# HGRN ahead of MoBA in the second mixer chain of a two-layer four-mixer decoder trunk, with longer delay estimates

## The chip, the cores and the metric

One core of a Trainium2 chip runs the whole program in one launch. The metric is the device time of one execution in microseconds (us). The kernel before takes 927.18 us, the median of three runs from 926.2 to 927.2 us.

Engine names as the profile uses them: PE is TensorE's matmul, PEld its weight load, DVE is VectorE, ACT is ScalarE, POOL is GpSimd, SP is SyncE.

## The reference

Two layers over 256 tokens of width 1024, float32, then a final RMSNorm. In each layer four token mixers of 4 heads of 64 work in parallel on projections of the same normed input, and each is projected, gated and summed:

```python
h = rms_norm(x, norm1_g[layer])
y_sb   = stick_breaking_attention(...)   # sigmoid attention with a reversed running product
y_rwkv = rwkv7_time_mix(...)             # S_t = S diag(w) + (S a) b^T + v k^T, per head
y_moba = moba_attention(...)             # one block of 256 here: causal softmax with partial rotary
y_hgrn = hgrn2_mixer(...)                # S_t = diag(f) S + (1-f) i^T, then RMSNorm and gate
for n, y_n in enumerate((y_sb, y_rwkv, y_moba, y_hgrn)):
    gate = sigmoid(h @ w_gate[n])
    merged += gate * (y_n @ w_branch[layer, n])
x = x + merged @ w_out[layer]
h2 = rms_norm(x, norm2_g[layer])
x = x + (silu(h2 @ w_ffn_gate) * (h2 @ w_ffn_up)) @ w_ffn_down
```

## The kernel before

Every large projection is done in split precision: `split` (lines 126 to 129) makes a rounded part `hi` of a float32 weight on ACT (line 128) and the remainder `lo` on DVE (line 129), and `mm3` (line 119) issues three fp32r matmuls for one product. A weight tile is 128x1024 (512 KB), loaded into one of four `raw` buffers by SP and split when its unit begins. The results of units go to the PSUM tiles `pa`, of which there are three.

The mixer phase of a layer, `phase`, gives PE two kinds of work. **Units** are projections, gates and branches, generators that yield every three or six matmuls. **Streams** are the mixers themselves, generators that issue a step of small matmuls and the vector work behind it and then yield a number: an estimate in ns of how long that vector work takes. `drive` (line 86) merges them. It counts the matmul time issued so far in `pe[0]`, and a stream whose step yielded `lat` is taken up again only when

```python
s[0] = pe[0] + lat * LATK        # LATK = 1.7
```

has been reached; until then the next units are issued. The estimates so set how many unit matmuls stand on PE between two steps of a mixer. They appear in no instruction.

There are two streams in a layer. The first, `rwkv` (line 471), makes scores by pairs of heads (`pair_scores`, line 535), inverts triangular blocks of 16 on DVE (`product`, lines 587 to 597), sends blocks through DRAM by two DMAs that ACT issues (`tri`, lines 600 and 603), solves the larger blocks with small matmuls, and applies the state in two chunks `c`. The second, `rest` (line 1085), runs stick-breaking attention `sba`, then `moba`, then `hgrn`. `hgrn` prepares keys and queries on DVE (lines 822 to 834) and goes through seven levels: at each, 16 or fewer small matmuls use `key` and `Q`, and DVE then updates `Q` (line 868, twice), `key` (line 869) and evicts the scores (line 876), before the next level's matmuls may begin. `moba` rotates q and k on DVE and POOL (lines 981 to 984), scores, softmax (lines 930, 991 to 998), transposes (`flip_att`, line 938) and weighs.

The order of the instructions on each engine is then made by the framework's scheduler from the order in which the program issues them. Each engine works its instructions off in that order.

Of the kernel before, what the change touches and what calls it, by code (L numbers as in the profile page):

```python
# [46 lines left out]
def trunk(ctx, tc, x, w_t, w_n, w_br, w_out, w_gu, w_dn, par, lora, rows, gains, consts, masks, out):  # L47
# [9 lines left out]
    def sb(tag, width, dt=F32):  # L57
        return mx.tile([128, width], dt, name=tag, tag=tag, bufs=NB[tag])

    def ps(tag):  # L60
        return psum.tile([128, 512], F32, name=tag, tag=tag, bufs=NB[tag])

    def g2d(t, a):
        return t.rearrange("p (a t) -> p a t", a=a)
# [130 lines left out]
    for i in range(20):  # L195
        nc.tensor.matmul(warm[:, 0:256], flat1[:, 0:128], flat1[:, 0:256], start=True, stop=True)
        if i in (8, 12):
            c = (i - 8) // 4
# [266 lines left out]
    def rwkv(m, l, yT):  # L465
# [100 lines left out]
        for c in range(2):  # L566
            LK.append(g2d(sb("b1", 1024), 4))
            pair_scores(kh, LK[c], c)
            yield 2400
        yield 500  # L570
        nc.vector.tensor_copy(yb.rearrange("p s t -> p (s t)")[:, 1::34],
                              xb.rearrange("p s t -> p (s t)")[:, 1::34])
        tmp = sb("xy", 512)[0:64]
# [157 lines left out]
        for c in range(2):  # L731
            p = ps("p1")
            for hp in range(2):
                for a in (2 * hp, 2 * hp + 1):
                    d = slice(a * 64, (a + 1) * 64)
                    mm_cols(p[:, d], LK[c][:, a, 0:128], vn[:, c, d], a == 0, c == 0 and a == 3)
                if c:
                    mm(p[:, hp * 128:(hp + 1) * 128], AR[:, 2 * hp + c, 0], st[:, hp], False, hp == 1)
            rh = sb("h1", 256)
            nc.scalar.copy(rh, p[:, 0:256])  # L740
            yield 1000
            p = ps("p1")
            for a in range(4):
                d = slice(a * 64, (a + 1) * 64)
                mm_cols(p[:, d], Y[c][:, a], rh[:, d])
            u = sb("h1", 256)
            nc.scalar.copy(u, p[:, 0:256])
            yield 1000
            if c == 0:
                p = ps("p1")  # L750
                for a in range(4):
                    o = p[hrow(a), (a // 2) * 64:(a // 2) * 64 + 64]
                    d = slice(a * 64, (a + 1) * 64)
                    mm(o, bkn[:, 0, d], u[:, d], True, False)
                    mm(o, bkn[:, 1, d], vn[:, c, d], False, True)
                st = g2d(sb("h1", 256), 2)
                nc.gpsimd.memset(st, 0.0)
                for hp in range(2):
                    for e in range(2):
                        s = hrow(e)  # L760
                        nc.vector.tensor_scalar(st[s, hp, s], p[s, hp * 64:(hp + 1) * 64], fac[s, hp:hp + 1],
                                                None, op0=OP.mult)
            p = ps("p1")
            for hp in range(2):
                for a in (2 * hp, 2 * hp + 1):
                    d = slice(a * 64, (a + 1) * 64)
                    mm_cols(p[:, d], LK[c][:, a, 128:256], vn[:, c, d], a == 0, False)
                if c:
                    mm(p[:, hp * 128:(hp + 1) * 128], AR[:, 2 * hp + c, 1], st[:, hp], False, False)
                for a in (2 * hp, 2 * hp + 1):  # L770
                    d = slice(a * 64, (a + 1) * 64)
                    mm_cols(p[:, d], LB[c][:, a, 128:256], u[:, d], False, a == 3)
            yv = g2d(p[:, 0:256], 4)
            mean = sm.tile([128, 4], F32, name="mean")
            nc.vector.tensor_reduce(mean, yv, axis=AX.X, op=OP.add)
            nc.vector.tensor_scalar(mean, mean, 1.0 / 64, None, op0=OP.mult)
            yc = sb("h1", 256)
            ycv = g2d(yc, 4)
            nc.vector.tensor_tensor(ycv, yv, bcast(mean, 64), op=OP.subtract)
            y2 = sb("h1", 256)  # L780
            nc.scalar.activation(y2, yc, AF.Square)
            var = sm.tile([128, 4], F32, name="var")
            nc.vector.tensor_reduce(var, g2d(y2, 4), axis=AX.X, op=OP.add)
            rsqrt_small(var, var, 1.0 / 64, 64e-5)
            nc.vector.tensor_tensor(ycv, ycv, bcast(var, 64), op=OP.mult)
            nc.vector.tensor_tensor(yc, yc, gnw, op=OP.mult)
            nc.vector.tensor_tensor(yc, yc, bonus[:, c], op=OP.add)
            nc.vector.tensor_tensor(yc, yc, g[:, c], op=OP.mult)
            ys.append(yc)
            yield 200  # L790
        yield 6000
        yT[1] = y_T(ys, "p1"), pe[0] + 2500

# [25 lines left out]
    def hgrn(m, l, yT):  # L819
# [22 lines left out]
        for lev in range(7):  # L842
# [19 lines left out]
            n = 4 * nb  # L862
# [36 lines left out]
        for t in range(2):  # L899
# [13 lines left out]
            nc.vector.tensor_tensor(y, y, gs[:, t], op=OP.mult)  # L913
            ys.append(y)
            yield 300
        yield 3500
        yT[3] = y_T(ys, "p2"), pe[0] + 2500

    def scores(q, k, t, mask):
# [57 lines left out]
    def moba(m, v, yT):  # L977
        r = []
        for u in m:
            o = g2d(sb("c2", 512), 2)  # L980
            nc.vector.stream_shuffle(o, g2d(u, 2), SWAP)  # L981
            nc.vector.tensor_tensor(o, o, over(sinT, 2), op=OP.mult)
            nc.gpsimd.tensor_tensor(g2d(u, 2), g2d(u, 2), over(cosT, 2), op=OP.mult)
            nc.vector.tensor_tensor(o, o, g2d(u, 2), op=OP.add)
            r.append(o)
        yield 5000
        po = ps("p3")
        for t in range(2):
            z, n = scores(r[0], r[1], t, cn[:, K_MO:K_MO + 128])
            mxs = sm.tile([128, 4], F32, name="mxs")  # L990
            nc.vector.tensor_reduce(mxs, z, axis=AX.X, op=OP.max)
            nc.vector.tensor_scalar(mxs, mxs, -0.125, None, op0=OP.mult)
            den = sm.tile([128, 4], F32, name="den")
            for a in range(4):
                nc.scalar.activation(z[:, a], z[:, a], AF.Exp, bias=mxs[:, a:a + 1], scale=0.125,
                                     accum_out=den[:, a:a + 1])
            nc.vector.reciprocal(den, den)
            nc.vector.tensor_tensor(z, z, bcast(den, n), op=OP.mult)
            yield 5000 + 2500 * t
            ts = []  # L1000
            flip_att(z, t, ts)
            yield 1200
            weigh(po, ts, t, v, 256)
        yT[2] = y_split(po), pe[0] + 2500
        yield 500
# [46 lines left out]
    def phase(hr, g, l, ws):  # L1052
        yT, gt, mg, mT = {}, {}, {}, {}
        streams, units = [], []
        yes = lambda: True

        def add(gen, ready=yes):
            units.append((ready, gen))

        def start(gen, pos):  # L1060
            def f():
                streams.append([pe[0] + 1500, gen, pos])
                streams.sort(key=lambda s: s[2])
                return
                yield
            add(f)

        vv = [sb("p", 512) for _ in range(2)]

        def use_v(t, p):  # L1070
            nc.scalar.copy(vv[t], p)

        h = norm_group(hr, g, ws, use_v)
        if l == 0:
            with tc.issue_after(tail[0].ins), tc.issue_after(tail[1].ins):
                setup()
            load_small()
        rm, sm_, mm_, hm = [], [], [], []
        for i in range(4):
            add(lambda i=i: rwkv_proj(h, l, i, rm))  # L1080
        start(rwkv_s(rm, l, yT), 0)
        for j in range(2):
            add(lambda j=j: copy_proj(h, l, 8 + 2 * j, sm_))

        def rest():
            yield from sba(sm_, vv, yT)
            while len(mm_) < 2:
                yield 2000
            yield from moba(mm_, vv, yT)
            while len(hm) < 4:  # L1090
                yield 2000
            yield from hgrn(hm, l, yT)
        start(rest(), 1)
        for j in range(2):
            add(lambda j=j: copy_proj(h, l, 12 + 2 * j, mm_))
        add(lambda: hgrn_proj(h, l, hm))
        cnt = [0, 0]
        for n in (0, 2, 3, 1):
            for f in range(2):
                add(lambda n=n, f=f: gate_unit(h, l, n, f, gt), lambda: len(gt) < NB["gt"] // 2)  # L1100
                add(lambda n=n, f=f: branch_unit(l, n, f, cnt, yT, gt, mg, mT),
                    lambda n=n, f=f: n in yT and yT[n][1] <= pe[0] and len(gt.get((n, f), ())) == 2)

        ahead = []

        def fetch():
            ahead.extend(prefetch([("gu", l, 0, c) for c in (0, 1)]))
            return
            yield
        units.insert(len(units) - UPRE, (lambda: 1 in yT and yT[1][1] <= pe[0], fetch))  # L1110
        drive(units, streams)
        return mT, ahead, flip_unit(1, mg, mT)
# [184 lines left out]
```

## Time and profile before

| | |
|---|---|
| runs | 926.2, 927.18, 927.2 us (median 927.18) |
| the profiled execution | 927.26 us, of which the span from first to last instruction is 925.5 us |
| PE busy | 905.9 us, 98% of the span, 5902 matmul passes |
| PEld | 758.4 us, 82% |
| DVE | 647.4 us, 70% |
| ACT | 475.2 us, 51% |
| POOL | 84.7 us, 9% |
| mean granted TensorE clock | 0.999 |
| DMA | 158.11 MB, mean 171 GB/s |

How to read it: busy shares are means over stages. The mixer phase of the first layer lies between about 17 and 254 us, that of the second between about 470 and 710 us; the merge and the FFN lie behind each. A row of the timeline gives start, duration, engine, line, operation, output and inputs, how many instructions are merged, and in brackets the idle time of the engine before it and what ended it. Matmuls overlap, so what one costs on PE is the distance from its start to the next start.

### The profile page before, as it was taken

Reading aid. Unit: us, or ns where it says so; the run is one execution under the profiler, and the core shown is the slowest. Engines: PE = TensorE matmul, PEld = TensorE weight load, DVE = VectorE, ACT = ScalarE, POOL = GpSimd, SP = SyncE. Lnnn points to the kernel's source line nnn. Section 1 sums busy time; section 2 is a strip of 40 time slices with the busy share of each in tenths; the row PEclk is TensorE's granted clock in tenths of the full one; section 3 lists DMA queues with packets and bytes.
Section 4 is the critical chain, followed back from the end, with each engine's and each line's share of the span. In section 5 each row is a group of like instructions: output and inputs, shape, how many; then the busy total and the mean of one; then the engine's idle time right before and its main releaser. Section 6 shows DMA issues by size and latency. Waiting matters only on the chain.

```text
span 925.5 us, 15008 instructions
## 1 busy us (share of the span) xinstructions
PE 905.9 (98%) x5902; PEld 758.4 (82%) x5902; DVE 647.4 (70%) x957; ACT 475.2 (51%) x726; POOL 84.7 (9%) x94
## 2 busy tenths in 40 slices
PE   8999999999999999999999999999999999999996
PEld 5999677778888888888889986777887888888885
DVE  6668877876766666668567778867778566666665
ACT  6564375355535455556345636644455445545453
POOL 3011100333000000000000201032230000000000
PEclk9999999999999999999999999999999999999999
DMA  8644453345864566667435544433467356656551
GB/s 308 222 147 152 121 169 128 102 155 176 266 205 138 181 190 196 182 204 267 144 115 160 161 138 144 142 123 124 131 211 253 112 184 204 189 184 195 182 182 46
DMA packets 50424, 158.11 MB, mean 171 GB/s; under 512 B 9393, under 2 KB 11953, under 8 KB 50354
## 3 DMA queue, kind: packets, MB, share of 16 engines
q1 hardware_dynamic: 43632, 155.19, 52.7%
q10 hardware_dynamic: 6722, 1.97, 0.9%
q8 instruction: 46, 0.75, 0.3%
q14 instruction: 24, 0.20, 0.1%
HBM read 154.91 MB, written 2.23 MB: 170 GB/s over the span
## 4 chain that ended last, share of the span: by engine, by line
PE 83%; DVE 8%; DMA 4%; issue 2%; ACT 2%; POOL 0%; SPq 0%; ACTq 0%; POOLq 0%; DVEq 0%
PE pa L80 58%; PE p L80 23%; DVE lo L129 2%; DMA raw<-in_w_n_dram 1%; PE p L89 1%; PE pa L89 1%; DMA h<-flat 1%; DMA tri<-yb 1%; DMA flat<-b 1%; DMA raw<-in_w_gu_dram 1%; DVE b L966 1%; ACT hi L128 0%; DVE b L542 0%; DVE c L129 0%; DVE c L981 0%
## 5 line engine op out<-in xcount | busy, mean ns | idle before, releaser
L129 DVE TENSOR_TENSOR lo<-raw,hi 128x1024 fp32r<-128x1024 f32 x268 | 330.2, 1237 | 162.6 <-ACT hi L128 159.7
L128 ACT CAST hi<-raw 128x1024 fp32r<-128x1024 f32 x268 | 279.1, 1048 | 238.5 <-PE pa L80 118.4
L80 PE MATMUL pa<-h,hi 128*128 128x256 f32 (+1 forms) x1280 | 277.9, 339 | 0.0
L80 PEld LDWEIGHTS pa<-h,hi 128*128 128x128 f32 x1280 | 215.9, 190 | 24.6 <-issue 2.0
L80 PE MATMUL pa<-hi,h 128*128 128x512 f32 x576 | 193.4, 400 | 2.2 <-DVE p L813 2.2
L80 PE MATMUL pa<-h,lo 128*128 128x256 f32 x960 | 179.9, 283 | 0.0
L80 PEld LDWEIGHTS pa<-h,lo 128*128 128x128 f32 x960 | 148.6, 191 | 7.0 <-issue 0.7
L80 PEld LDWEIGHTS pa<-hi,h 128*128 128x128 f32 x576 | 108.1, 188 | 27.6 <-DVE p L813 3.0
L80 PE MATMUL p<-hi,c 128*128 128x512 f32 (+1 forms) x352 | 113.4, 394 | 0.0
L80 PE MATMUL pa<-lo,h 128*128 128x512 f32 x288 | 112.7, 391 | 0.0
L80 PEld LDWEIGHTS p<-hi,c 128*128 128x128 f32 x352 | 66.1, 189 | 15.2 <-DVE c L129 0.6
L80 PE MATMUL p<-lo,c 128*128 128x512 f32 (+1 forms) x176 | 69.2, 393 | 0.0
L80 PEld LDWEIGHTS pa<-lo,h 128*128 128x128 f32 x288 | 54.2, 188 | 10.0 <-issue 0.3
L263 POOL TENSOR_TENSOR rs<-rs,half 128x1 f32<-128x1 f32 x10 | 6.0, 595 | 471.6 <-DVE rs L262 471.6
L80 PE MATMUL pa<-hi,y 128*128 128x512 f32 x128 | 43.9, 399 | 0.0
L80 PE MATMUL p<-hi,b 128*128 128x512 f32 x128 | 41.5, 396 | 0.2 <-DVE b L129 0.2
L80 PEld LDWEIGHTS p<-lo,c 128*128 128x128 f32 x176 | 33.1, 188 | 6.8
L1034 POOL TENSOR_TENSOR p<-p,gt 128x512 f32<-128x512 f32 x16 | 31.2, 1973 | 54.3 <-DVE gt L1032 54.3
L340 DVE TENSOR_TENSOR gt<-gt,pa 128x256 f32<-128x256 f32 x80 | 33.1, 414 | 0.0
L128 ACT CAST c<-xy 128x512 fp32r<-128x512 f32 x20 | 12.4, 620 | 39.2 <-DVE xy L1137 39.2
L339 ACT COPY gt<-pa 128x256 f32<-128x256 f32 x80 | 29.3, 366 | 0.0
L80 PEld LDWEIGHTS pa<-hi,y 128*128 128x128 f32 x128 | 24.0, 188 | 6.3 <-issue 1.0
(276 smaller groups left out, 936.5 us busy)
## 6 DMA issues: line engine op xcount, KB each, us to landing
raw<-in_w_gu_dram SPq DMA_DIRECT2D x88, 512.0 KB, 3.7
raw<-in_w_n_dram SPq DMA_DIRECT2D x80, 512.0 KB, 3.5
raw<-in_w_dn_dram SPq DMA_DIRECT2D x44, 512.0 KB, 3.5
raw<-in_w_t_dram SPq DMA_DIRECT2D x40, 512.0 KB, 3.6
raw<-in_w_br_dram SPq DMA_DIRECT2D x16, 512.0 KB, 3.6
raw<-in_w_out_dram SPq DMA_DIRECT2D x16, 512.0 KB, 4.4
b<-in_gains_dram SPq DMA_DIRECT2D x4, 512.0 KB, 5.2
flat<-b ACTq DMA_DIRECT2D x4, 256.0 KB, 3.2
```

Source lines behind the costliest of these rows:

```text
L80: nc.tensor.matmul(o, l, r, start=start, stop=stop)
L89: nc.tensor.transpose(o, i, ident)
L128: a = nc.scalar.copy(dst[0], src)
L129: return a, (eng or nc.vector).tensor_tensor(dst[1], src, dst[0], op=OP.subtract)
L263: nc.gpsimd.tensor_tensor(dst, dst, half[:, :dst.shape[-1]], op=OP.pow)
L339: nc.scalar.copy(dst, p[:, 256:512])
L340: nc.vector.tensor_tensor(dst, dst, p[:, 0:256], op=OP.add)
L966: nc.vector.tensor_tensor_scan(kb, kb, reset[t][:, ::-1], 1.0, op0=OP.mult, op1=OP.add)
L1034: e.tensor_tensor(mg[f, t], mg[f, t], g, op=OP.add)
```

## The change

Five delay estimates are altered, `rest` runs `hgrn` before `moba`, and the projections, gates and branches of the two change places likewise.

```diff
@@ rwkv: scores of k (LK), two steps
         for c in range(2):
             LK.append(g2d(sb("b1", 1024), 4))
             pair_scores(kh, LK[c], c)
-            yield 2400
-        yield 500
+            yield 3200
@@ rwkv: application of the state, chunks c = 0, 1
             ys.append(yc)
-            yield 200
+            yield 1500 - 1300 * c
         yield 6000
@@ hgrn: before the last transposes
             ys.append(y)
             yield 300
-        yield 3500
+        yield 4300
@@ moba: after the softmax of query half t
-            yield 5000 + 2500 * t
+            yield 6800 + 1500 * t
             ts = []
             flip_att(z, t, ts)
@@ phase
         def rest():
             yield from sba(sm_, vv, yT)
+            while len(hm) < 4:
+                yield 2000
+            yield from hgrn(hm, l, yT)
             while len(mm_) < 2:
                 yield 2000
             yield from moba(mm_, vv, yT)
-            while len(hm) < 4:
-                yield 2000
-            yield from hgrn(hm, l, yT)
         start(rest(), 1)
+        add(lambda: hgrn_proj(h, l, hm))
         for j in range(2):
             add(lambda j=j: copy_proj(h, l, 12 + 2 * j, mm_))
-        add(lambda: hgrn_proj(h, l, hm))
         cnt = [0, 0]
-        for n in (0, 2, 3, 1):
+        for n in (0, 3, 2, 1):
```

No instruction is added or taken away on PE, DVE, ACT, POOL or SP; the lines of the changed kernel from 570 on are one lower than those of the kernel before. What moves is best seen at three places. In these rows a number behind a name tells buffers apart, `lo<-raw,hi` is the DVE part of a weight's split, and `h_1078` and `h_1120` are the blocks that come back from DRAM for the inversion.

The first place is DVE in the first layer, from the arrival of the blocks for the inversion to the evictions of the scores of k, chunk 0 (line 542). Before:

```order
L129 TENSOR_TENSOR lo<-raw,hi 128x1024
L981 STREAM_SHUFFLE c_1150<-p 128x512
L981 STREAM_SHUFFLE c_1155<-p 128x512
L542 COPY_PREDICATED b_1122<-mk,p_1123 128x2x256
L542 COPY_PREDICATED b_1122<-mk,p_1124 128x2x256
L982 TENSOR_TENSOR c_1150<-c_1150,cn 128x512
```

Now:

```order
L570 COPY yb<-h_1078 64x8
L591 TENSOR_TENSOR xy<-yb,h_1078 64x4x4 x2
L594 TENSOR_REDUCE h_1260<-xy 64x4x2 x2
L591 TENSOR_TENSOR xy<-h_1260,yb 64x4x4 x2
L812 TENSOR_TENSOR p<-p,pa 128x256
L823 TENSOR_SCALAR c_1114<-p,lb_129,lb_128 128x256 x2
L825 TENSOR_SCALAR p<-p,lb_128,lb_127 128x256 x2
L828 TENSOR_TENSOR c_1119<-p,c_1114 128x512
L833 TENSOR_TENSOR b_1121<-p 64x2x256
L542 COPY_PREDICATED b_1080<-mk,p_1081 128x2x256
L542 COPY_PREDICATED b_1080<-mk,p_1082 128x2x256
L833 TENSOR_TENSOR b_1121<-p 64x2x256
```

HGRN's preparation (L823 to L833) stands where the shuffles of MoBA's rotation stood, and all of it is behind the copy that waits for the blocks.

The second place is DVE a little further on, around the last level of the inversion (the products of 64x512). Before:

```order
L542 COPY_PREDICATED b_1172<-mk,p_1173 128x2x256
L542 COPY_PREDICATED b_1172<-mk,p_1174 128x2x256
L592 TENSOR_TENSOR xy<-yb,h_1120 64x512
L595 TENSOR_REDUCE h_1227<-xy 64x64
L592 TENSOR_TENSOR xy<-h_1227,yb 64x512
L129 TENSOR_TENSOR lo<-raw,hi 128x1024
L595 TENSOR_REDUCE yb<-xy 64x8x8
L129 TENSOR_TENSOR lo<-raw,hi 128x1024
L813 TENSOR_TENSOR p<-p,pa 128x256
```

Now:

```order
L542 COPY_PREDICATED b_1155<-mk,p_1157 128x2x256
L591 TENSOR_TENSOR xy<-yb,h_1078 64x512
L871 TENSOR_TENSOR tot_1377<-tot_1326 128x64
L594 TENSOR_REDUCE h_1260<-xy 64x64
L129 TENSOR_TENSOR lo<-raw,hi 128x1024
L837 COPY dg<-p_1192 128x8
L867 TENSOR_TENSOR b_1121<-b_1121,p 64x2x128 x2
L868 TENSOR_TENSOR c_1114<-c_1114,p 128x256
L875 COPY_PREDICATED h_1203<-mk,p_1205 128x128
L591 TENSOR_TENSOR xy<-h_1260,yb 64x512
L129 TENSOR_TENSOR lo<-raw,hi 128x1024
L594 TENSOR_REDUCE yb<-xy 64x8x8
```

HGRN's update behind level 0 (L867, L868) now stands inside the inversion, behind one of its two large products; the matmuls of level 1 need it.

The third place is ACT around the DMA that writes the inverted blocks (`tri<-yb`), which waits for DVE's last reduction into `yb`. Before:

```order
L600 DMA tri<-yb 64x256
L811 COPY p<-pa 128x256
L812 ACTIVATE p<-pa 128x256
L603 DMA h_1356<-tri 128x8x16
L811 COPY p<-pa 128x256
L812 ACTIVATE p<-pa 128x256
L128 CAST hi<-raw 128x1024
```

Now:

```order
L950 COPY p<-pa 128x512
L599 DMA tri<-yb 64x256
L128 CAST hi<-raw 128x1024
L602 DMA h_1412<-tri 128x8x16
L128 CAST hi<-raw 128x1024 x2
L1011 ACTIVATE gt<-pa 128x512 x2
L128 CAST hi<-raw 128x1024 x4
```

The evictions of HGRN's token-major projection out of `pa` (L811, L812) stood behind both DMAs; they have moved far ahead of them, and splits and gate sigmoids stand there now.

## Rows read from the trace of the kernel before

**Rows 1.** The page, part 1: busy time of each engine.

```profile
PE 905.9 (98%) x5902; PEld 758.4 (82%) x5902; DVE 647.4 (70%) x957; ACT 475.2 (51%) x726; POOL 84.7 (9%) x94
```

**Rows 2.** Windows: stretch, length, busy PE, PEld, DVE, ACT, POOL, clock, DMA share, GB/s.

```profile
93.00:133.00 40.00, 36.74 (x189) 28.00 (x185) 33.31 (x64) 21.82 (x41) 4.50 (x5) 1.00 0.48 147
202.00:254.00 52.00, 52.00 (x235) 42.90 (x234) 36.84 (x41) 28.74 (x37) 9.45 (x5) 1.00 0.67 210
```

**Rows 3.** Waits of PE from 40 to 254 us: total, times, longest.

```profile
PE p L89 <- DVE c L998: 1.4, 1, 1.4
PE pa L80 <- DVE p L813: 1.1, 1, 1.1
PE p L80 <- DVE h L761: 1.0, 1, 1.0
PE p L80 <- DVE b L542: 0.7, 1, 0.7
```

**Rows 4.** Timeline of PE in the second layer: the rows behind its three longest waits.

```profile
551.58 0.70 PE L80 MATMUL p<-b,c 64*128 64x256 f32 x2 [0.72 <-DVE b L542]
...
564.34 0.50 PE L80 MATMUL pa<-hi,h 128*128 128x512 f32 x1 [1.09 <-DVE p L813]
...
572.64 0.63 PE L89 MATMUL p<-cn,c 128*128 128x128 f32 x4 [1.20 <-DVE c L998]
```

**Rows 5.** Timeline of PE between 90 and 112 us.

```profile
90.16 0.28 PE L80 MATMUL pa<-h,lo 128*128 128x256 f32 x1
90.28 0.40 PE L80 MATMUL pa<-h,hi 128*128 128x256 f32 x2
...
92.66 1.13 PE L80 MATMUL p<-b,c 64*128 64x256 f32 x8
...
109.60 0.39 PE L80 MATMUL pa<-lo,h 128*128 128x512 f32 x1
109.83 0.39 PE L80 MATMUL pa<-hi,h 128*128 128x512 f32 x1
111.30 0.50 PE L80 MATMUL pa<-hi,h 128*128 128x512 f32 x1 [1.08 <-DVE p L813]
```

**Rows 6.** Timeline of DVE: the inversion, HGRN's preparation, two level updates.

```profile
93.38 0.17 DVE L571 COPY yb<-h 64x8 f32<-64x8 f32 x1 [0.87 <-DMA h<-flat]
...
102.64 1.21 DVE L129 TENSOR_TENSOR lo<-raw,hi 128x1024 fp32r<-128x1024 f32 x1
103.78 1.34 DVE L542 COPY_PREDICATED b<-mk,p 128x512 f32<-128x512 uint8 x2
105.01 1.04 DVE L592 TENSOR_TENSOR xy<-yb,h 64x512 f32<-64x512 f32 x1
106.09 0.68 DVE L595 TENSOR_REDUCE h<-xy 64x64 f32<-64x512 f32 x1
...
116.42 0.68 DVE L607 TENSOR_TENSOR xy<-h,mk 128x512 f32<-128x512 f32 x1
...
140.85 0.73 DVE L824 TENSOR_SCALAR c<-p,lb,lb 128x256 f32<-128x256 f32 x2
...
144.15 0.43 DVE L872 TENSOR_TENSOR tot<-p 128x256 f32<-128x256 f32 x1
...
153.30 1.29 DVE L868 TENSOR_TENSOR b<-b,p 64x256 f32<-64x256 f32 x2
154.62 0.43 DVE L869 TENSOR_TENSOR c<-c,p 128x256 f32<-128x256 f32 x1
...
165.96 0.85 DVE L869 TENSOR_TENSOR c<-c,tot 128x256 f32<-128x256 f32 x1
```

**Rows 7.** Timeline of ACT: the write of the inverted blocks, and what stood behind.

```profile
109.60 0.49 ACTq L600 DMA_DIRECT2D tri<-yb  x1
110.13 0.37 ACT L811 COPY p<-pa 128x256 f32<-128x256 f32 x1 [3.78 <-DVE yb L595]
```

**Rows 8.** Timeline of POOL beside the last row of rows 6.

```profile
164.85 1.68 POOL L721 TENSOR_TENSOR c<-c,rws 128x256 f32<-128x256 f32 x2
```

## The prediction

> **What bounds the kernel now.** First the page's list of engines: PE is busy for 905.9 us, 98% of the span, DVE for 70%, ACT for 51% [rows 1]. The change gives PE the same matmuls in another order, so time can come only from PE's holes or from new ones. Second, the windows: from 202 to 254 us, where units alone are left, PE is busy for all of 52.00 us; from 93 to 133 us, where the inversion runs beside MoBA, it lacks 3.3 us of 40, while DVE is busy for 33.31 us of these 40 [rows 2]. The holes lie where DVE is fullest. Third, the waits of PE: in the first layer four are worth naming, 1.4 us for MoBA's softmax, 1.1 us for a `pa` tile, 1.0 us for the state, 0.7 us for an eviction of k's scores [rows 3]; the second layer has three of the same, 1.2, 1.1 and 0.7 us [rows 4]. Idle time understates a wait, because a matmul's end is modelled: around the `pa` wait the starts are 1.47 us apart, where two 512-column matmuls otherwise stand 0.23 us apart, so 1.24 us are lost for 1.08 us shown [rows 5]. I add 0.16 us to each wait.
>
> **What the change removes.** A wait goes where more unit matmuls stand ahead of the waiting step, or where its producer moves.
> - Eviction (L542). The step of k's chunk 1 is put off from 2400 to 3200 units of estimate, by 0.8 x 1.7 = 1.4 us of PE work, more than the 0.7 + 0.16 us lost.
> - Softmax (L998). The estimate of half 0 goes from 5000 to 6800, 3.1 us more cover for 1.4 + 0.16 us lost; MoBA also leaves the stretch in which DVE is fullest.
> - `pa` tile (L813). ACT stood in front of the DMA that writes the inverted blocks for 3.78 us, until DVE had them, and the evictions of HGRN's projection stood behind that DMA [rows 7]. They now stand ahead of it.
> - State (L761), first layer. Chunk 0's estimate goes from 200 to 1500, 2.2 us of cover for 1.0 + 0.16 us.
>
> In the first layer that is 4.2 + 4 x 0.16 = 4.9 us, in the second 3.0 + 3 x 0.16 = 3.5 us, 8.4 us together. The bounds of this term are 0 and 8.4 us.
>
> **What it adds.** HGRN's preparation and levels 0 to 4 now share DVE with the inversion. I count both engines from the copy that ends the wait for the blocks, 93.38 us [rows 6]; the DMA behind it is issued from the same place as before.
>
> *DVE up to the update that level 1 needs*, in the new order: the copy and six small operations 0.7 us; an eviction L812 0.34; the preparation 3.3 (L824 to L872 lie between 140.85 and 144.15); two evictions 1.23 (103.78 to 105.01); `lo` of y 0.6; three `lo` of weights at 1.14 (102.64 to 103.78); the small remainder of the inversion 1.8; two more evictions 1.23; the first large product 1.08 (105.01 to 106.09), its reduction 0.7, small totals 0.3; the update 0.16 + 1.3 + 0.43 [rows 6]. The sum is 16.6 us, so the update is done at about 110.0 us.
>
> *PE up to level 1.* k's scores of chunk 0 stood at 92.66 us [rows 5]; ahead of them 48 matmuls of 0.23 us have taken the place of 96 of 0.12 us, so 92.2 us. Then come two bursts of small matmuls (2.1 us), 36 unit matmuls of 256 columns at 0.12 us (4.6 with the changes of kind), chunk 1 (1.1), 18 more (2.4), level 0 (0.95), 36 more and three of 512 columns (5.3): 108.6 us. PE waits **1.4 us** for level 1.
>
> *Level 2.* PE needs 0.4 us for level 1 and 21 x 0.23 = 4.8 us for units, 5.2 us. DVE has ahead of the next update an eviction (0.35), the second product (1.08), two `lo` (2.28), a reduction (0.7), totals (0.65), then the update (1.3): 6.4 us. That is 1.2 us more than PE; consecutive rows of DVE overlap a little, so I take **1.0 us**.
>
> *Level 3.* `yb` is complete at about 113.2 us. Before, the write left at 109.60 and the blocks were used at 116.42 [rows 6, 7], 6.8 us later; the same trip ends at 120.0 us at the latest. DVE stands before L606 with level 2's update behind it (0.6 + 1.3): 121.9 us at the latest, against PE at about 121.4. I take **0.2 us** for this. Level 4 and later have 0.2 to 1 us to spare by the same count.
>
> So about 2.6 us per layer are new, 5.2 us together; bounds: 0 (DVE arrives 2 us sooner), and 7.6 us per layer (below). MoBA now ends alone among units, with long estimates; its softmax is costed at nothing, since 66 unit matmuls of gates and branches (15 us at 0.23 us) cover its longer half; without them it would cost the 1.4 us it costs now. The 4300 before HGRN's transposes and the new order of branches move only into stretches where PE has no hole [rows 2], and are costed at nothing. SP issues the same loads in the order of the units, four buffers ahead; POOL's rotation products wait for DVE's shuffles later, and nobody needs them for 10 us.
>
> **The sum** against the profiled execution, 927.26 us (0.08 us above the median): 927.26 - 8.4 + 5.2 = **924.1 us**.
>
> One rule speaks against the order. First the row: a level update's product on `key` took 0.85 us at 165.96 us, while POOL ran two additions from SBUF (164.85 us, 1.68 us), and 0.43 us at 154.62 us without such company [rows 6, 8]. The Trainium skill (SBUF — State Buffer, Who interferes with whom) says that a DVE instruction with two SBUF inputs contends with a GpSimd instruction that reads SBUF, and that whoever is first blocks the other for its whole length. By that rule POOL's two gate products (L813), which now run just ahead of HGRN's preparation, could hold DVE once more for about one of them, and the sum would be some 1.4 us higher, 925.5 us. The two rows agree with the rule in kind; no row shows these two side by side.
>
> **The rivals.**
> - *DVE keeps up.* If the blocks land 2 us sooner relative to PE, or ACT feeds the splits better, no level waits: 927.26 - 8.4 = 918.9 us. For it: the scheduler put only what level 1 needs ahead of the second product. Against it: from 93.38 us on the new order gives DVE no hole for 16 us. Chance 0.17.
> - *The waits change places.* New waits equal the old ones, 4.2 us per layer, if DVE is 1.6 us later than I count (a late landing, or four of its products doubled). 927.3 us, with 925.5 to 929 around it. Chance 0.20.
> - *DVE becomes the bound: slower.* If all three products of an update take 0.85 instead of 0.43 us, as at 165.96 us [rows 6], each of four updates costs 1.26 us more and PE, waiting at each level, pays all of it: 5.0 + 2.6 = 7.6 us per layer, 927.26 - 8.4 + 15.2 = 934.1 us. It decides from 1.6 us per layer on, and is slower by what can be measured from 2.5 us on. For it: DVE's load from 93 to 133 us rises to nearly all of the 40 us (33.31, less MoBA's rotation and softmax, plus the preparation and five updates). Against it: POOL has little to do there, 4.5 us [rows 2]. Chance 0.13.
> - *The change does not do what it says.* The order shows that it does; what could fail is only that an estimate moves a step onto another step. That is in the second rival.
>
> **How the numbers follow.** A measurement of this kernel tells 0.2% from no change, 1.85 us. The forecast has 0.50: its own range is 921.5 to 926.5 us, of which about 0.07 lies above 925.4 us. Faster: 0.43 + 0.17 = 0.60. The same: 0.07 + 0.20 = 0.27. Slower: 0.13. The range that should hold 8 in 10 goes from 919.0 to 928.5 us: it reaches the edge of the first rival, takes in the second, and leaves out most of the third.
>
> **What would show it.** The waits of PE on L998, L813 and L542 gone, and L761 with them; in their place waits for DVE lines 867 or 868 at HGRN's levels 1 and 2, near 109 and 115 us and again some 453 us later; L606 on DVE waiting for the second DMA. PE's busy share a little up at the same 5902 passes. The forecast is wrong if waits on these levels exceed 4 us per layer or are absent, if a wait on ACT's copies appears in the state's chunks of the second layer, or if units wait for `lo`.

## The result and the profile after

The changed kernel takes **934.3 us** (median of five runs, 932.3 to 936.0) against 927.2 us of the kernel before beside it: a ratio of 1.0060, 95% interval 1.0042 to 1.0078. It is slower, where 924.1 us was forecast, and lies outside the range.

The profiled execution took 934.3 us, its span 932.5 us. Page, part 1, of the kernel after:

```profile
PE 909.5 (98%) x5902; PEld 760.7 (82%) x5902; DVE 647.2 (69%) x957; ACT 475.2 (51%) x726; POOL 88.9 (10%) x94
```

Beside [rows 1] the work is the same: the same passes, DVE within 0.2 us. Two windows, columns as in [rows 2]:

```profile
93.00:133.00 40.00, 35.37 (x382) 29.66 (x381) 34.21 (x73) 15.99 (x22) 2.31 (x3) 1.00 0.42 130
202.00:254.00 52.00, 52.00 (x245) 42.84 (x244) 35.05 (x37) 31.49 (x46) 9.82 (x5) 1.00 0.63 201
```

The units' stretch still has no hole. From 93 to 133 us PE lacks 4.6 us of 40 instead of 3.3. Waits of PE, first layer (40 to 258 us), total, times and longest, to be held against [rows 3]:

```profile
PE p L80 <- DVE c L868: 4.3, 3, 2.3
PE p L89 <- ACT xy L679: 0.7, 1, 0.7
PE p L80 <- ACT h L739: 0.4, 1, 0.4
PE pa L80 <- DVE p L1029: 0.2, 1, 0.2
PE p L80 <- DVE b L542: 0.2, 1, 0.2
```

The same in the second layer (470 to 718 us), against [rows 4]:

```profile
PE p L80 <- DVE c L868: 3.7, 3, 1.8
PE p L80 <- ACT xy L679: 1.4, 1, 1.4
PE p L80 <- ACT c L938: 0.3, 1, 0.3
```

All four waits of [rows 3] are gone; the 0.2 us on L542 belongs to an earlier step, at 85.26 us. In their place stand HGRN's levels, three times in each layer, and the copies of the solved blocks (L679). Timeline of PE at the three levels, each with the unit matmul ahead of it:

```profile
110.83 0.39 PE L80 MATMUL pa<-hi,h 128*128 128x512 f32 x1
112.91 0.46 PE L80 MATMUL p<-b,c 128*32 128x32 f32 x32 [1.69 <-DVE c L868]
...
117.97 0.39 PE L80 MATMUL pa<-hi,h 128*128 128x512 f32 x1
118.73 0.46 PE L80 MATMUL p<-b,c 128*32 128x32 f32 x32 [0.38 <-DVE c L868]
...
123.79 0.39 PE L80 MATMUL pa<-hi,h 128*128 128x512 f32 x1
126.43 0.46 PE L80 MATMUL p<-b,c 128*32 128x32 f32 x32 [2.26 <-DVE c L868]
```

By the distance of the starts, less the usual 0.23 us, the first layer loses 1.85, 0.54 and 2.42 us there, the second 1.71, 0.53 and 1.91 us. (All losses below are counted so, against the distance that the same two matmuls have where nothing waits, and only those above 0.3 us are named.) The timeline of DVE, beside [rows 6], shows why the third is long:

```profile
118.73 1.26 DVE L129 TENSOR_TENSOR lo<-raw,hi 128x1024 fp32r<-128x1024 f32 x1
124.36 0.69 DVE L606 TENSOR_TENSOR xy<-h,mk 128x512 f32<-128x512 f32 x1 [4.37 <-DMA h<-tri]
124.97 0.86 DVE L867 TENSOR_TENSOR b<-b,tot 64x256 f32<-64x256 f32 x2
125.86 0.43 DVE L868 TENSOR_TENSOR c<-c,tot 128x256 f32<-128x256 f32 x1
```

DVE stands still for 4.37 us before the product that needs the second DMA, in the stretch where it was thought to be full, and the update that PE wants is behind it. The time of that DMA is on the page, part 6 (issues, KB, median us to landing), first of the kernel before, then of the kernel after:

```profile
h<-tri ACTq DMA_DIRECT2D x2, 64.0 KB, 2.8
```

```profile
h<-tri ACTq DMA_DIRECT2D x2, 64.0 KB, 5.0
```

In the changed kernel SP issues a weight load 0.9 us behind this read. Timeline of ACT and of SP, first layer:

```profile
119.09 0.38 ACTq L602 DMA_DIRECT2D h<-tri  x1
...
120.02 0.33 SPq L133 DMA_DIRECT2D raw<-in_w_n_dram  x1
```

**Part of the 7 us between these two executions is not the change's.** Rows of PE before the mixers, where both kernels have the same instructions, of the kernel before and then of the kernel after:

```profile
4.34 2.11 PE L199 MATMUL p<-b,h 1*128 1x512 f32 x4
```

```profile
4.34 3.78 PE L199 MATMUL p<-b,h 1*128 1x512 f32 x4
```

Four matmuls of 512 columns take 3.78 us at the lower clock level (1.2 GHz) and 2.11 at the upper (2.4 GHz). The trace records the full clock from 4.64 us on in the kernel before and from 13.05 us on in this execution; up to there PE had worked without a pause from 1.45 us on in both. The mixers start 2.6 us later for it. Of the span's 7.0 us the first mixer phase has 1.4 and the second 3.0; the FFNs are alike.

### The profile page after: what moved, and what is told of

It reads as the page before. It is cut to its first block, busy times and chain, and to the rows that moved or that the text cites. A ratio compares the mean times of both kernels' runs of the same rounds, so it can differ in the third digit from the quotient of the medians.

```text
span 932.5 us, 15006 instructions
## 1 busy us (share of the span) xinstructions
PE 909.5 (98%) x5902; PEld 760.7 (82%) x5902; DVE 647.2 (69%) x957; ACT 475.2 (51%) x726; POOL 88.9 (10%) x94
## 4 chain that ended last, share of the span: by engine, by line
PE 80%; DVE 10%; DMA 4%; issue 3%; ACT 2%; POOL 1%; SPq 0%; ACTq 0%; POOLq 0%; DVEq 0%
PE pa L80 56%; PE p L80 22%; DVE lo L129 2%; DMA h<-tri 1%; PE p L89 1%; PE pa L89 1%; ACT hi L128 1%; DMA tri<-yb 1%; POOL hvar L263 1%; DMA raw<-in_w_n_dram 1%; DVE b L542 1%; DVE xy L591 1%; DVE b L867 1%; DMA raw<-in_w_out_dram 0%; DMA cn<-in_consts_dram 0%
```

## The experiments

To keep that start out of the count, the table has, beside the medians, the length of each mixer phase in the profiled execution: from the start of PE's 200th matmul to that of its 2200th, and from the 3000th to the 5000th (the stretch between the two, and the one behind them, are alike within 0.1 us in all runs). The kernel before has 280.4 and 274.5 us.

| kernel | median us | beside it, before | ratio, 95% interval | phases us |
|---|---|---|---|---|
| after | 934.3 | 927.2 | 1.0060, 1.0042 to 1.0078 | 281.7, 277.5 |
| after_again | 936.9 | 929.3 | 1.0075, 1.0052 to 1.0098 | 284.4, 277.3 |
| est_alone | 928.9 | 929.4 | 0.9988, 0.9974 to 1.0001 | 278.6, 275.9 |
| order_alone | 931.1 | 929.4 | 1.0014, 0.9999 to 1.0029 | 281.4, 276.1 |
| read_late | 931.7 | 929.4 | 1.0017, 1.0001 to 1.0033 | 282.1, 275.6 |
| copies_act | 932.5 | 929.4 | 1.0030, 1.0016 to 1.0044 | 283.9, 276.4 |
| lk_old | 928.4 | 929.3 | 0.9992, 0.9975 to 1.0009 | 279.1, 275.3 |
| est_tri_pool | 930.1 | 929.3 | 1.0011, 0.9995 to 1.0026 | 280.4, 275.1 |
| levels_first | 931.6 | 929.3 | 1.0015, 1.0001 to 1.0029 | 279.3, 274.4 |
| read_on_sp | 932.6 | 928.7 | 1.0044, 1.0028 to 1.0059 | 282.0, 275.4 |
| lk_old_sp | 925.8 | 928.7 | 0.9974, 0.9958 to 0.9990 | 277.1, 273.1 |
| lk_old_edge | 926.7 | 928.7 | 0.9980, 0.9968 to 0.9992 | 278.3, 274.1 |
| both_on_sp | 928.1 | 929.6 | 0.9978, 0.9965 to 0.9991 | 279.6, 275.7 |

**The changed kernel again (after_again).** No edit.

> The changed kernel once more, beside the kernel before on the same chip. Theory (the 2.6 us that the profiled execution lost before the mixers, where the granted clock reached full speed at 13.05 us instead of 4.64 us, belong to the single execution and not to the change; the rest, 1.4 + 3.0 us, lies in the two mixer phases): the median is 933.5 to 935 us, 4.5 to 5 us above a kernel before that now also starts slowly in most executions (929.4 us in the last comparison). Rival (the late clock belongs to the change): the difference is 7 us, the kernel before at 927.2.

Each side is half right. The kernel before is at 929.3 us here, 2.1 us above its first median, as the theory of the start has it. Its executions here have no trace, so that most of them start late is inferred: 20 of the 29 lie between 929.0 and 930.6 us, seven between 926.3 and 927.5. But the change costs 7.6 us all the same, as the rival has it, and the phases grow by 4.1 and 2.8. Two things in the first layer are new against the first profile. Timeline of ACT:

```profile
85.26 3.88 ACTq L548 DMA_DIRECT2D flat<-b  x2
89.23 1.05 ACT L128 CAST hi<-raw 128x1024 fp32r<-128x1024 f32 x1 [5.01 <-DVE b L542]
93.79 0.69 ACTq L564 DMA_DIRECT2D h<-flat  x1
...
96.60 1.10 ACT L938 COPY c<-p 128x512 f32<-128x512 f32 x2
```

ACT may issue the first read (L564) only when the write has landed. It does so 4.65 us after the row of the writes ends (85.26 + 3.88); in the kernel before 2.86 us (82.68 + 3.88 to 89.42). Behind it on ACT are a split, HGRN's four evictions and the copies L938, and PE waits for these copies. Over the step of small matmuls that needs them PE takes 3.32 us here and 1.61 us where nothing waits (both_on_sp), so 1.7 us are lost. The second is the clock, in windows of 1 us (the third number from the end):

```profile
129.00:130.00 1.00, 1.00 (x4) 0.76 (x4) 1.00 (x2) 0.70 (x2) 0.00 (x0) 0.51 0.00 0
130.00:131.00 1.00, 1.00 (x4) 0.81 (x3) 1.00 (x3) 0.84 (x1) 0.00 (x0) 0.50 0.32 41
131.00:132.00 1.00, 1.00 (x3) 0.77 (x3) 1.00 (x2) 0.00 (x0) 0.00 (x0) 0.50 0.85 283
132.00:133.00 1.00, 1.00 (x5) 0.78 (x4) 0.94 (x3) 0.00 (x0) 0.00 (x0) 0.79 0.53 213
```

After the holes at L938 and at levels 1 to 3 the granted clock falls to its lower level; the four windows lack 0.49 + 0.50 + 0.50 + 0.21 = 1.7 us. It did so in copies_act too (0.75 from 130 to 135 us), not in the first profile.

The wait on L938 (L939 where lines are one higher) goes with the write ahead of it. ACT issues the first read in 18 layers of the profiles with HGRN first. In the twelve where it stood for the write for 3.7 us or more, PE lost 0.8 to 2.0 us on these copies; in the six where it stood for 3.1 us or less, it lost nothing that counts.

**The estimates alone (est_alone)** and **the order alone (order_alone).** The kernel before with the five estimates of the diff; the changed kernel with the five old ones.

> The kernel before with the five longer estimates alone; MoBA stays ahead of HGRN. Theory (the estimates buy what was forecast, the new order is what costs): the waits of PE on L998 (1.4 and 1.2 us), L542 (0.7 and 0.7) and L761 (1.0, first layer) go, the one on the pa tile (L813, 1.1 and 1.1) stays, no wait at HGRN's levels: 927.2 - 5.8 = 921.4 us, 920.5 to 924. Rival (longer estimates push the mixers' steps into each other in any order, the order is innocent): 927 to 934 us, with new waits on the state's or HGRN's steps.

> The changed kernel with the old five estimates: HGRN ahead of MoBA, nothing else. Theory: HGRN's levels 1 to 3 wait as in the changed kernel (about 4.8 us in the first layer, 4.2 in the second by the distance of the starts), and k's scores or the state wait again: 934.3 + 0 to 3 us, so 934 to 938. Rival (the estimates are what costs): within 1 us of 927.

Neither theory is right; 928.9 us lies in the range of est_alone's rival, 931.1 us in no range of order_alone. Alone the estimates gain 0.5 us and the order costs 1.6, neither beyond the error; together they cost 7.1 to 7.6. In est_alone the waits on L998, L542 and L761 went as counted, but the one for the `pa` tile doubled (2.49 and 2.41 us), a level of HGRN waited for 1.05 us (L868, at 199.38 us), and the clock fell once, from 565.9 us on, behind the second of the `pa` waits. In order_alone the levels cost only 1.55 and 2.6 us. So the cost is in the meeting of one of the estimates with the order.

**Which estimate (lk_old).**

```diff
             pair_scores(kh, LK[c], c)
-            yield 3200
+            yield 2400
+        yield 500
```

> The changed kernel with one estimate put back, that of k's scores (2400 per chunk and 500 behind instead of 3200 per chunk). Theory (the inversion, started 1.9 us of PE work later, is what keeps DVE from HGRN's updates; with the old estimates in the new order the levels waited only 1.55 + 2.6 us): waits at the levels fall from 4.8 + 4.2 to about 1.6 + 2.6 us, the wait on the scores' second eviction comes back (0.7 + 0.9): 934.3 - 4.8 + 1.6 = 931.1 us, 930 to 932. Rival (the other estimates make the levels wait): 933.5 to 936 us.

It is this one: 936.9 to 928.4 us, more than the theory's 3.2. The levels lose 1.1 and 2.9 us instead of 4.5 and 5.3. PE's waits in the first layer, of after_again and then of lk_old (lines one higher):

```profile
PE p L80 <- DVE c L868: 4.0, 3, 2.1
PE p L80 <- ACT c L938: 1.2, 1, 1.2
PE p L89 <- ACT xy L679: 0.7, 1, 0.7
PE p L80 <- ACT h L739: 0.4, 1, 0.4
```

```profile
PE p L80 <- ACT c L939: 1.1, 1, 1.1
PE p L80 <- DVE c L869: 0.8, 2, 0.6
PE p L80 <- DVE b L542: 0.7, 2, 0.5
```

The forecast took the longer estimate as cover, worth 0.86 us per layer at L542. It bought that, and put the inversion later against everything else: in the first layer the write of `tri` leaves at 117.25 us in after_again, at 115.97 in lk_old, and its round trip up to the product that needs it lasts 8.5 us (to 125.78) against 5.2 (to 121.20); in the second layer 9.3 against 7.0. Why the trip is shorter in lk_old is not shown: in both kernels one load is in flight when the read is issued and one more is issued behind it. In DVE's order the copies of the solved blocks stand behind the last step of HGRN's norm in after_again and ahead of it in lk_old.

**The read's product out of the way (read_late).** Both L606 are put behind level 2's key update on DVE (`issue_after` fixes the order of two instructions of one engine):

```diff
@@ rwkv: before and around the product of L606
         yield 2500
+        while l not in mark:
+            yield 1000
         for c in range(2):
             y = g2d(sb("xy", 512), 4)
+            with tc.issue_after(mark[l].ins):
...
@@ hgrn: the key update of a level
-            nc.vector.tensor_tensor(kv[:, :, 0], kv[:, :, 0], tv[:, :, 1:2].to_broadcast([128, n, hb]), op=OP.mult)
+            ku = nc.vector.tensor_tensor(kv[:, :, 0], kv[:, :, 0], tv[:, :, 1:2].to_broadcast([128, n, hb]), op=OP.mult)
+            if lev == 2:
+                mark[l] = ku
```

> The changed kernel with the two L606 products, which wait for the second DMA of the inversion, held behind the key update of HGRN's level 2 on DVE; PE's order is the same word for word. Theory (DVE stood 4.37 us before L606 with an update behind it that PE wanted): the wait of PE at level 3 goes in both layers, 2.42 + 1.91 = 4.3 us, 934.3 - 4.3 = 930.0 us, 929.3 to 931. Rival (DVE is full, so the next level pays what this one is spared): 933 to 934.5 us, with a new wait of 1.5 to 2 us at level 4 or 5.

Against after_again 5.3 us less, against the first runs 2.6. In the trace level 3 no longer waits, but level 4 now does, 0.91 and 0.72 us, and PE loses 1.9 and 0.9 us on L938. The mechanism of the theory is shown, with over a third of the gain given back as the rival has it; 931.7 us lies between the two ranges.

**The copies (copies_act).**

```diff
-                (nc.scalar.copy if u else nc.vector.tensor_copy)(Y[c][L64, u::2, H64], g2d(p[hrow(u), 0:128], 2))
+                nc.scalar.copy(Y[c][L64, u::2, H64], g2d(p[hrow(u), 0:128], 2))
```

> The changed kernel with the two copies of the solved block that DVE made (L679, one per chunk) given to ACT, which makes the other two; all other engines keep their order word for word. Theory (the copies are queued on DVE behind HGRN's output norm, which waits for POOL): PE's wait on them, 0.88 + 1.54 us by the distance of the starts, goes but for two more ACT copies of some 0.3 us in line, so 934.3 - 2.0 = 932.3 us, 931.7 to 933. Rival (ACT is late by itself, its splits stand in front): 934 to 935 us, the wait the same under ACT's name.

As the theory had it in both layers: no wait on L679 is left, and 932.5 us lies in its range, though that is counted from the first median and not from after_again's; its phases are 0.5 and 0.9 us shorter than after_again's. The cause, in the timeline of DVE, of POOL and of ACT in the changed kernel:

```profile
158.74 0.42 DVE L912 TENSOR_TENSOR h<-h,p 128x256 f32<-128x256 f32 x1
159.07 0.17 DVE L262 TENSOR_SCALAR hvar<-hvar 128x4 f32<-128x4 f32 x1
159.14 0.69 DVE L983 TENSOR_TENSOR c<-c,p 128x512 f32<-128x512 f32 x1
160.73 0.42 DVE L911 TENSOR_TENSOR h<-p,hvar 128x256 f32<-128x256 f32 x1 [0.90 <-POOL hvar L263]
161.19 0.43 DVE L912 TENSOR_TENSOR h<-h,p 128x256 f32<-128x256 f32 x1
161.53 1.22 DVE L129 TENSOR_TENSOR lo<-raw,hi 128x1024 fp32r<-128x1024 f32 x1
162.67 0.47 DVE L679 COPY xy<-p 64x128 f32<-64x128 f32 x2
```

```profile
159.32 1.38 POOL L263 TENSOR_TENSOR hvar<-hvar,half 128x4 f32<-128x4 f32 x1 [1.28 <-DVE hvar L262]
```

```profile
162.98 0.46 ACT L679 COPY xy<-p 64x128 f32<-64x128 f32 x2 [3.58 <-DVE xy L679]
```

DVE's two copies, 0.47 us together, stand behind HGRN's output norm, which stands for POOL's power of 512 numbers, and behind one `lo`. ACT's two copies, for which PE waits by name, stand for DVE's.

**The order on DVE set by hand (levels_first).** By the same means as in read_late, both L606 stand behind the key update of level 3, and the products of the inversion's last level behind that of level 0:

```diff
+            while (l, 0) not in mark:
+                yield 500
+            with tc.issue_after(mark[l, 0].ins):
+                product(t4, blk(yb, 0, 0), blk(xb, 0, 1))
+                product(blk(yb, 0, 1), t4, blk(yb, 1, 1))
```

> The changed kernel with two fixed orders on DVE: the inversion's last two large products behind HGRN's level 0 key update, and the two L606 products behind HGRN's level 3 key update; PE's order is word for word the same. Theory (DVE did the right work in the wrong order): the waits at level 1 (1.85 + 1.71 us) and level 3 (2.42 + 1.91) go, 934.3 - 7.5 = 926.8 us, 926 to 928.5 with up to 1.7 us given back where rwkv's solve is later. Rival (DVE is full over the whole stretch, each wait only moves on): 931 to 934 us, with waits at level 4, at the solve or on a merge product (L1029).

The profiled execution, which happens to have the early clock (2.12 us for the row above) and short writes (2.2 us from the issue of the write of `tri` to its landing), took 926.0 us; the median is 931.6 us, in the rival's range. Even there level 1 still loses 0.93 and 0.81 us and level 2 now 1.77 in each layer: the wait moved one level on. The rival is right for these two levels; only level 3, where DVE stood, is gained.

**The write and read by POOL (est_tri_pool).** est_alone, with this edit and the same for the read of `cb`:

```diff
-        nc.scalar.dma_start(tri.rearrange("p (s t) -> p s t", s=16), yb)
+        nc.gpsimd.dma_start(tri.rearrange("p (s t) -> p s t", s=16), yb)
```

> The kernel before with the five longer estimates, and the two DMAs of the inversion's result (write and read-back of tri) issued by POOL instead of ACT; PE's and DVE's orders are word for word those of the estimates alone. Theory (ACT stands before the write and HGRN's evictions of pa stand behind it): the pa wait of 2.49 + 2.41 us by the distance of the starts goes, 928.9 - 4.5 = 924.4 us, 923.5 to 926. Rival (POOL issues the two transfers later than ACT, the solve's products then hold DVE and PE waits there): 928 to 931 us.

930.1 us lies in the rival's range. The `pa` wait is nearly as long as in est_alone (2.21 and 2.28 us), so ACT's standing made little of it. ACT now evicts early; DVE's product on the same tile comes 4.5 us after that, in its place behind the inversion's last products. ACT and DVE, first layer:

```profile
108.32 0.39 ACT L811 ACTIVATE p<-pa 128x256 f32<-128x256 f32 x1
...
113.21 0.40 DVE L812 TENSOR_TENSOR p<-p,pa 128x256 f32<-128x256 f32 x1
```

And DVE now stands 4 us before L606, with `lo` of a unit behind it, for which PE waits (1.75 and 1.59 us). That is a unit, not the solve that the rival named.

**The read by SP (read_on_sp).** SP issues three weight loads, then the read-back, then the fourth:

```diff
-        nc.scalar.dma_start(cb, bass.AP(tensor=tri.tensor, offset=tri.offset, ap=[[16, 128], [2048, 8], [1, 16]]))
+        nc.sync.dma_start(cb, bass.AP(tensor=tri.tensor, offset=tri.offset, ap=[[16, 128], [2048, 8], [1, 16]]))
```

> The changed kernel with the read-back of the inverted blocks (h<-tri) issued by SP, behind three of the weight loads and ahead of the fourth, instead of by ACT; PE's and DVE's orders are word for word the same. Theory (the read-back takes 4.6 to 6.1 us because the fourth load is issued 0.4 to 1.1 us behind it and runs beside it; before, it had 2.6 to 3.0 us with no load issued until it had landed): the trip falls to 2.6 to 3.5 us, DVE stands before L606 for 2 us instead of 4.2, PE's wait at level 3 falls from 2.3 to 3.1 us to under 1 us in each layer, and the time is 3 to 4 us under the changed kernel's, 932 to 934 us. Rival (the trip is long by its 1024 small blocks or the load already in flight): trip 4.5 us or more, time within 1 us of the changed kernel's 934.3 to 936.9.

Half right. The read takes 4.1 and 3.9 us instead of 4.6 and 6.1, level 3 loses 1.50 and 0.87 us instead of 2.29 and 3.08, and the time is within the range; but one load is still in flight when the read is issued, one more is issued behind it, and the read is over the 2.6 to 3.5 us of the theory.

**Both reads by SP (lk_old_sp, both_on_sp).** The same edit for `cb` and for `xb` (`h<-flat`), once with the old estimate of k's scores, once with the changed kernel's 3200. In both the scheduler also reorders DVE: the inversion's second small remainder stands ahead of HGRN's first eviction, and its last product ahead of level 0's update.

> The changed kernel with the old estimate of k's scores, and both reads of the inversion (h<-flat and h<-tri) issued by SP; PE's order is that of the old estimate alone, word for word. Theory: ACT no longer stands before the first read with HGRN's evictions and the copies L939 behind it, so PE's wait on L939 (1.8 us in the first layer, 1.3 in the second by the distance of the starts) goes, and loads are issued behind the reads, so that the trips are short and the wait at level 3 of the second layer (1.8 us) goes: 928.4 - 4.5 = 923.9 us, 923 to 926. Rival (SP stands before the reads and the weight loads behind it come late): 927 to 931 us, with waits of units on the splits (L128, L129).

> The changed kernel, with its longer estimate of k's scores, and both reads of the inversion (h<-flat and h<-tri) issued by SP, as in the run with the old estimate and both reads on SP (925.8 us); PE's order is the changed kernel's, word for word. Theory (the longer estimate costs 8 us only through the transfers: ACT standing before the first read, loads beside the trips, DVE standing before the second): the waits on L938 and at level 3 go, level 2 waits some 1.3 us as with the old estimate, no fall of the clock: 926 to 928.5 us. Rival (DVE is full and the longer estimate leaves its updates less cover, whatever the transfers do): the waits at levels 1 to 3 stay above 3 us per layer, the copies L679 still make PE wait 0.9 and 1.5 us, 930 to 934 us.

Both times lie in the ranges of the theories, and in both runs the waits on L938 (L939) and at level 3 are gone. The waits that are left are not all the theory's: in lk_old_sp level 2 waits for 1.3 us, but in both_on_sp it is level 1, and the copies L679 make PE wait as the rival has it. With the estimate that cost 8 us the kernel is now at 928.1 us, and PE's order is the changed kernel's, word for word. By the medians that is 0.2% under the kernel before; by the phases of its profiled execution it is 0.4 us above it, so the two are best called level. Page, part 6, and the waits of PE in the first layer, both of both_on_sp:

```profile
h<-tri SPq DMA_DIRECT2D x2, 64.0 KB, 2.2
```

```profile
PE p L80 <- DVE c L868: 1.6, 1, 1.6
PE p L89 <- ACT xy L679: 0.7, 1, 0.7
PE p L80 <- DVE b L542: 0.5, 2, 0.3
```

While SP stands before a read it issues no load, so none is in flight when the read starts, and the next are queued behind it; ACT goes on with the evictions meanwhile. PE waits for no split of a weight. Left are level 1 (1.78 and 1.77 us), level 2 in the second layer (0.70) and L679 (0.87 and 1.53). How much of the gain is the transfers' and how much the reordered DVE's isn't told apart; read_on_sp, where DVE's order is the changed kernel's, shows the part of the one read. **lk_old_sp, 925.8 us, beats both kernels** (0.26% under the one before beside it; its phases are 3.3 and 1.4 us shorter).

**The old estimate with the read by SP and its product put back (lk_old_edge).** lk_old, `cb` by SP, and the edge of read_late.

> The changed kernel with the old estimate of k's scores, the read-back issued by SP ahead of the third load, and the two products that use it held behind HGRN's level 2 key update on DVE. Theory: PE's wait at level 3 of the second layer (1.8 us) goes and nothing else moves: 928.4 - 1.8 = 926.6 us, 925.5 to 927.5. Rival (the wait moves on to level 4 or the solve): 928 to 929 us.

926.7 us, and level 3 of the second layer no longer waits, as the theory had it. Something else moved as well: the loss on L939 is 0.5 and 0.4 us smaller. And since the read also changes its queue here, its share and the fixed order's are not told apart.

## Why the prediction was wrong

- **The removed waits: right.** L998, L813, L542 (second step) and L761 are absent from the waits after. By the distances they were worth 8.4 us, as counted. order_alone shows that the longer estimates were needed for part of it: there L998 waits 1.43 us in the first layer. For the `pa` tile the reason given, ACT's stand before the write, is not what est_tri_pool shows: without that stand 2.2 us of the wait were left, because DVE's product on the tile came late. In the new order that product moved ahead as well.
- **Level 1 and level 2: right in place and near in size.** 1.85 and 1.71 us for the 1.4, 0.54 and 0.53 for the 1.0.
- **Level 3: the step that failed.** It stood at 0.2 us and measured 2.42 and 1.91. The rest of that count came true: `yb` at 113.2 us and PE at 121.4 are 115.8 and 124.0 with the 2.6 us of the start, and the write left at 115.70 and PE was ready at 124.02. But the trip of the blocks was taken from [rows 6, 7] as 6.8 us with the words "at the latest", and it takes 8.7 us (115.70 to 124.36), 8.2 in the second layer. The part that grew is the read, 5.2 and 4.8 us instead of 2.6 and 3.0. Before, one load was in flight when the read was issued and no other came until it had landed; in the new order a second load is issued 0.9 us behind it. With no load in flight and the next ones behind it on its queue the read takes 2.2 us (both_on_sp). That this company alone sets the length is not shown: lk_old and order_alone have the same company, and their four reads take 3.2 to 5.0 us.
- **What was costed at nothing: the other step that failed.** In the first profile L679 0.88 + 1.54 us, L739 0.61, a merge product (L1029) 0.43 in each layer, and L938 0.76 in the second; in the second profile L938 1.7 in the first layer instead. copies_act shows the cause of L679, and lk_old_sp and both_on_sp that of L938: there SP stands for the write, and the wait is gone. "The DMA behind it is issued from the same place as before" was true and beside the point: the write ahead of that DMA took longer in the layers where L938 made PE wait. What makes L739 and L1029 late was not tested.
- **The sum, by what was measured:** 927.3 - 8.4 + 9.0 (levels) + 4.7 (L679, L739, L1029, L938) + 2.6 (start) = 935.2 us, against 934.3. Against the forecast of 924.1 us that is 3.8 us more for the levels, 4.7 for what stood at nothing, and 2.6 for the start. Two of the signs named in the prediction appeared: the levels wait for more than 4 us per layer (4.8 and 4.2), and ACT's copies make PE wait, though not in the state's chunks of the second layer.
- **The eviction's estimate** was credited with 0.86 us per layer as pure cover. With the new order it was the part that made the change slow (lk_old); with the old order it cost nothing that can be measured (est_alone).
- **The rivals.** The second had the nearest mechanism: it named a late landing as a way to new waits of 4.2 us per layer, and the levels lost 4.8 and 4.2. Its time, 927.3 us, lacks what was costed at nothing and the start. The third gave 934.1 us, and that it meets the measured time is luck: all 14 products of the updates on `key` (L868) take 0.42 or 0.43 us in the kernel after, not 0.85. That POOL's company is dear shows elsewhere: the products of MoBA's rotation on DVE (L982, now L981), all four of which now run beside POOL's, take 1239 ns on average where they took 837 (two beside POOL's, 995 ns each, and two alone, 679). Lines of DVE by form, before and after:

```profile
L982 DVE TENSOR_TENSOR c<-c,cn 128x512 f32<-128x512 f32 x4 | 3.3, 837 | 0.0
```

```profile
L981 DVE TENSOR_TENSOR c<-c,cn 128x512 f32<-128x512 f32 x4 | 5.0, 1239 | 0.0
```

The rule of the Trainium skill that the prediction weighed (SBUF — State Buffer, Who interferes with whom) agrees with these rows in kind. They are not the products for which the prediction weighed it, and their 1.7 us are busy time of DVE, of which no run shows what part reaches PE.

- **The start** was taken as fixed, from one execution. The medians of the kernel before lie between 927.2 and 929.6 us in the five comparisons; a range that allowed for such a move would have reached 2.6 us higher, and still not 934.

## What to carry to other kernels

A delay estimate that gives one step cover puts off every step behind it in the same stream: look at what those will then meet, not only at the wait that it removes. A small DMA on the path took up to 2.7 times as long beside loads as without them here, so a duration from the trace is no upper bound once the loads around it move. Where such a read is on the path, try to issue it from the queue of the loads, ahead of them, and not from an engine whose evictions PE needs. On an engine that works in order, the cost of a late operand is the work queued behind it: find that work before pricing the wait at nothing, even where the engine's busy share says that it is full.

## What the runs showed of the hardware

- The read of `tri`, 64 KB, took 2.2 to 2.4 us with no weight load in flight at its issue (both_on_sp, lk_old_sp), 2.6 to 3.2 with one in flight and none behind it (the kernel before, est_alone), and 3.2 to 4.1 with one in flight and one issued 0.7 to 1.1 us behind it on its own queue (read_on_sp, lk_old_edge). With one in flight and one issued 0.4 to 1.2 us behind it on the other queue it took 4.6 to 6.1 (the changed kernel, twice), 4.9 to 5.3 (read_late, copies_act) and 3.2 to 5.0 (order_alone, lk_old); with that load 1.6 us behind, 3.1 to 4.1 (levels_first). What spreads it within one company is open. The Trainium skill (DMA: Bandwidth & Descriptors, Issuing engines are not separate DMA queues) says that DMAs of different engines run on the same 16 DMA engines and interleave; that the read is longer beside loads of another queue agrees with it.
- The write of the first blocks kept ACT or SP from the read for 2.7 to 2.9 us in six of six layers with MoBA first, and with HGRN first for 2.8 to 4.9 us. In both_on_sp SP issued no load behind the write until it had landed, and it was still 4.8 and 4.0 us, so loads issued behind it are not the whole reason. What the reason is stays open.
- The clock rose to its upper level at 4.6 us in two profiled executions (before, levels_first) and between 12.7 and 14.1 us in the twelve others, with the same instructions up to there. In the changed kernel's first profile that cost 2.6 us of the span.
- Behind four holes of PE, 0.5 to 2.7 us long, between 95 and 128 us the clock fell to its lower level in two of the profiled executions with HGRN first, at a cost of 1.7 us; in read_on_sp, with holes at the same four places, it did not. In est_alone it fell behind one hole of 2.4 us.
